# Turning attention probabilities outside TensorE: 32x32 blocks on VectorE and a trip through DRAM in place of identity products, in a two-layer hybrid encoder

## The chip, the core and the metric

The kernel runs on one core of one Trainium2 chip. Times are device microseconds (us) of one execution of the whole program. The core has five engines that run beside each other: TensorE (PE, matrix products; its weight loads are shown as PEld), VectorE (DVE), ScalarE (ACT), GpSimd (POOL) and SyncE (SP). SP does no arithmetic here: it issues nearly all DMAs, in the order of the program, so that a DMA that has to wait for something holds up every DMA behind it on that queue.

## The reference

Two layers. Each has a token mixer and a convolutional MLP, with RMSNorm before each and a residual add behind. SEQ is 256, D_MODEL 1024, everything float32. What matters here is the attention inside the mixer: 12 heads of width 128 in three groups of four, group `g` with window and dilation (128,1), (512,4), (2048,16). The groups' results are combined by their softmax denominators, which is the same as one softmax over the keys of all three groups.

```python
u, q, k, v, g_pool, g_attn = jnp.split(xn @ w_in, SPLITS, axis=-1)
...
logits = jnp.einsum('bqhd,bqkhd->bhqk', qb, kb, preferred_element_type=jnp.float32) * scale
logits = logits + bias.astype(jnp.float32)[None, :, None, :]
logits = jnp.where(valid[None, None], logits, NEG_INF)
lse = jax.nn.logsumexp(logits, axis=-1)
p = jnp.exp(logits - lse[..., None]).astype(vb.dtype)
o = jnp.einsum('bhqk,bqkhd->bqhd', p, vb)
...
wts = jax.nn.softmax(jnp.stack(lses, axis=0), axis=0)
attn = jnp.einsum('gbsh,gbshd->bshd', wts, jnp.stack(outs, axis=0).astype(jnp.float32))
...
merged = jax.nn.sigmoid(g_pool) * (pool_out @ w_a) + jax.nn.sigmoid(g_attn) * (attn_out @ w_b)
return merged @ w_o
```

## The kernel before

**Products and weights.** Most products are made in three parts: both operands are split into a high and a low half in TensorE's fast fp32r type, and high*high, low*high and high*low are summed. Weights come from DRAM in loads of 1 MB into three buffers (`RAW = 3`; `Weights.load`, line 134). Each load is cut into two pieces of 128x1024. ScalarE makes a piece's high half (line 197) and VectorE its low half (line 198); five split pieces can be live (`BUFS = 5`). `Weights.get` asks for the pieces in the order of use, up to `LOOK = 3` ahead of TensorE. `W.loads_behind[n]` puts the issue of load n behind a named DMA on SP's queue, and `W.queue_behind` puts the splitting of some pieces behind named instructions on ScalarE and VectorE.

**Stages of a layer.** (1) values `v`; (2) the pooling branch's input and its projection; (3) queries and keys, six column pairs (`PAIRS`) of four projections each, by `proj` and `two_sums` (matmuls on line 520); (4) the pooling branch times `w_a`, by tokens: `by_tokens(po2, 4)` for two halves of the columns, four pieces each (matmuls on line 644, copied to `pa` on line 1099); (5) two gates for the pooling branch (`gate()`, `by_tokens(x2, 4)`, tanh on line 1107); (6) two gates for attention, each followed by `by_tokens(at2, 2, 2)` with `w_b`; the merged rows are turned to channels by `to_chunks` (lines 663 to 677): a VectorE transpose of 32x32 blocks (line 667), a DMA to DRAM (line 669), four DMAs back (line 671), and the split into halves (line 676); (7) the product with `w_o` (lines 562 to 564) with the residual and the norm; (8) the MLP.

**Attention.** Head `hh` of all three groups is handled at once, in three functions. `scores(hh)` makes for each half `t` of the tokens 128 x 512 logits: 256 columns for the first group (line 985, three parts) and 128 for each of the others (line 990, plain float32). VectorE adds the bias (line 996) and finds the maximum (line 1001), ScalarE makes the exponentials (line 1004), VectorE divides (lines 1006 and 1007). The result `probs[hh, t]` has queries on partitions. `turn(hh)` brings the keys onto partitions: TensorE multiplies each 128x128 block with the identity (line 1019, eight for a head); from PSUM, ScalarE copies the first group's part to `pth` in fp32r (line 1020), VectorE makes its low half `ptl` (line 1025), and the other groups' part is copied to `pt` in float32 (lines 1022 and 1024). `weigh(hh)` multiplies with the values (line 1036 in three parts, line 1040 in plain float32) and splits the result into `at2` (lines 1045 and 1046).

**Where attention stands.** These functions are not a stage of their own. A list `steps` holds twelve of them, in the order scores a, turn a, scores b, weigh a, turn b, weigh b for the pairs of heads (0, 1) and (2, 3). `step()` runs the next one; I call each place where it is called a visit. There is a visit after every second projection of the last three column pairs in stage 3 (six visits), and after six of the eight pieces in stage 4.

**Buffers that the change touches.** Tiles with one tag share memory, one after another. `ybig` holds in turn half of the pooled input (`pl2`), `pa`, and a piece of `w_up`; `xn` holds the other half of `pl2`, the low halves of queries and keys (`qkl`), and the normed rows; `gates` holds `vl` and then the tanh rows `th`; `gain` holds a norm's gain, sent to all partitions by a 512 KB DMA.

Of the kernel before, what the change touches and what calls it, by code (L numbers as in the profile page):

```python
# [10 lines left out]
F32 = mybir.dt.float32  # L11
# [5 lines left out]
P = 128  # L17
D = 1024
S = 256
DEPTH = 2  # L20
KD = D // P
HD = 128
HPG = 4
# [203 lines left out]
def encoder(ctx, tc, x, w_in, w_pool, pool_scale, w_a, w_b, w_o, norm1, norm2, w_up, conv_w,  # L227
            conv_b, w_down, rel_bias, norm_f, onehot, edges, out):
    nc = tc.nc
    const = ctx.enter_context(tc.tile_pool(name="const", bufs=1))  # L230
    wpool = ctx.enter_context(tc.tile_pool(name="weights", bufs=1))
    big = ctx.enter_context(tc.tile_pool(name="big", bufs=1))
    sm = ctx.enter_context(tc.tile_pool(name="small", bufs=2))
    acc = ctx.enter_context(tc.tile_pool(name="acc", bufs=4, space=bass.MemoryType.PSUM))
    mmp = ctx.enter_context(tc.tile_pool(name="mmp", bufs=4, space=bass.MemoryType.PSUM))
    dram = ctx.enter_context(tc.tile_pool(name="dram", bufs=1, space=bass.MemoryType.DRAM))


    W = Weights(tc, wpool, big)

    def cols(w, c0):

        src = w[:, c0 : c0 + 256].rearrange("(k p) c -> p k c", p=P)
        return W.add(
            src, (8, 256), [((lambda t, j=j: t[:, :, j * P : (j + 1) * P]), (8, P)) for j in (0, 1)]
        )
# [10 lines left out]
    first_up = []  # L257
    for l in range(DEPTH):
        for g in range(NG):
            c0 = C_V + g * 512  # L260
            slots = (("m2", 0, 2), ("m2", 1, 2), ("ybig",), ("at2",)) if g == 0 else ()
            for j in range(2):
                tag = "k1" if l == 0 and g == 1 and j == 0 else None
# [25 lines left out]
        for j in range(2):  # L289
            tag = None if j else "k1"  # L290
            W.use(rows(w_up[l], j * 512, 4, 0, 512, tag), slots[2 * j : 2 * j + 2])
        for f in range(0, NF, 2):
            a = cols(w_up[l], f * P) if f >= ENTRY else []
            g = cols(w_up[l], DFF + f * P)
# [10 lines left out]
    def gain(src):  # L305
        g = sm.tile([P, D], F32, tag="gain", bufs=1, name="gain")
        nc.sync.dma_start(out=g, in_=src.partition_broadcast(P))
        return g

    ident = const.tile([P, P], F32, name="ident")  # L310
# [324 lines left out]
    def v_tile():  # L635
        return acc.tile([P, 512], F32, tag="acc", name="v_ps")

    def v_sum(ps, x2, t, n, piece, last=3):


        _, (wh, wl) = piece
        passes = [(0, wh, 0), (0, wl, 0), (1, wh, 0), (0, wh, 1), (0, wl, 1), (1, wh, 1)]
        for m, (part, w, j) in enumerate(passes):
            nc.tensor.matmul(  # L644
                ps, x2[:, 2 * n + j, part, t, :], w[:, j, :], start=(n + m == 0),
                stop=(n == last and m == 5),
            )

    def by_tokens(x2, n, at_once=1, then=None):

        ps = [mmp.tile([P, 512], F32, tag="mm", name="t_ps") for _ in range(2)]
        for i0 in range(0, n, at_once):
            held = [W.get() for _ in range(at_once)]
            for t in range(2):
                for i, piece in enumerate(held, i0):
                    v_sum(ps[t], x2, t, i, piece, n - 1)
            for i, _ in held:
                W.free(i)
            if then:
                then()  # L660
        return ps
# [17 lines left out]
    def two_parts(tag, name):  # L679


        return big.tile([P, KD, 2, 2, P], F32R, tag=tag, name=name)
# [174 lines left out]
    for l in range(DEPTH):  # L857
# [4 lines left out]
        v = big.tile([P, 2, 2 * 512], F32, tag="v1", name="v")  # L862
# [16 lines left out]
        if l == 0:  # L879
            with tc.manual_schedule():  # L880
                begun = begin_values_of_x()
            x2 = first_values(*begun, keep_values)
        else:
            for g in range(NG):
                held = begun[0] if g == 0 else [W.get() for _ in range(4)]
                for t in range(2):
                    if g + t == 0:
                        ps = begun[1]
                    else:
                        ps = v_tile()  # L890
# [6 lines left out]
        if l == 0:  # L897
            load_params()
            with tc.issue_after(W.behind[1].ins):
                bias = build_bias()  # L900
                next(bias)
        g2 = gain(norm2[l])


        pl2 = [
            big.tile([P, KD // 2, 2, 2, P], F32R, tag=tag, name="pl2") for tag in ("ybig", "xn")
# [2 lines left out]
        for gi in range(3, -1, -1):  # L909
# [12 lines left out]
            while sh < w:  # L922
# [3 lines left out]
                    out=nxt[:, :, 0:n], in0=cur[:, :, 0:n], in1=cur[:, :, sh : sh + n]  # L926
# [7 lines left out]
            if hw > 1:  # L934
# [5 lines left out]
                out=pd, in0=cur[:, :, o : o + S], scalar=1.0 / w, in1=u[:, :, PAD : PAD + S],  # L940
# [35 lines left out]
        q = big.tile([P, NH - HPG, 2, P], F32, tag="q1", name="q")  # L976
        kk = big.tile([P, NH - HPG, 2, P], F32, tag="k1", name="k")
        at2 = big.tile([P, HPG, 2, 2, P], F32R, tag="at2", name="at2")
        probs, ptiles = {}, {}

        def scores(hh):
            for t in range(2):
# [26 lines left out]
                )  # L1009
                probs[hh, t] = p  # L1010

        def turn(hh):
            pth = sm.tile([P, 2, 2, P], F32R, tag="pth", bufs=1, name="pth")
            ptl = sm.tile([P, 2, 2, P], F32R, tag="us", name="ptl")
            pt = sm.tile([P, 2, 2, P], F32, tag="pt", bufs=1, name="pt")
            for t in range(2):
                ps = acc.tile([P, 4, P], F32, tag="acc", name="pt_ps")
                for b in range(4):
                    nc.tensor.transpose(ps[:, b, :], probs[hh, t][:, b * P : (b + 1) * P], ident)  # L1019
                nc.scalar.copy(out=pth[:, :, t, :], in_=ps[:, 0:2, :])  # L1020
                if t == 0:
                    nc.scalar.copy(out=pt[:, :, t, :], in_=ps[:, 2:4, :])
                else:
                    nc.vector.tensor_copy(pt[:, :, t, :], ps[:, 2:4, :])
                nc.vector.tensor_sub(
                    out=ptl[:, :, t, :], in0=ps[:, 0:2, :], in1=pth[:, :, t, :].bitcast(F32)
                )
            ptiles[hh] = pth, ptl, pt

        def weigh(hh):  # L1030
            pth, ptl, pt = ptiles[hh]
            ps = acc.tile([P, 2, P], F32, tag="acc", name="o_ps")
            for kc in range(2):
                c = slice(hh * P, (hh + 1) * P)
                for m, (a, b) in enumerate(((vh, pth), (vh, ptl), (vl, pth))):
                    nc.tensor.matmul(ps, a[:, kc, c], b[:, kc], start=(kc + m == 0), stop=False)  # L1036
            for g in (1, 2):
                hd = (g - 1) * HPG + hh
                for t in range(2):
                    nc.tensor.matmul(  # L1040
                        ps[:, t, :], v[:, t, hd * P : (hd + 1) * P], pt[:, g - 1, t, :],
                        start=False, stop=(g == 2 and t == 1),
                    )
            oh, ol = at2[:, hh, 0], at2[:, hh, 1]
            nc.scalar.copy(out=oh, in_=ps)
            nc.vector.tensor_sub(out=ol, in0=ps, in1=oh.bitcast(F32))

        steps = []
        for pair in ((0, 1), (2, 3)):
            a, b = pair  # L1050
            steps += [(scores, a), (turn, a), (scores, b), (weigh, a), (turn, b), (weigh, b)]

        def step():
            if steps:
                f, hh = steps.pop(0)
                f(hh)


        for m, c in enumerate(PAIRS):
            if m == 1:  # L1060
                po2 = two_parts("m2", "po2")
# [5 lines left out]
            for n in range(4):  # L1067
# [3 lines left out]
                hd = 2 * c + n % 2  # L1071
                scale = HD**-0.5 if n < 2 else 1.0
                if hd < HPG:
                    hi, lo = ((qh, ql) if n < 2 else (kh, kl))
                    nc.scalar.mul(out=hi[:, hd], in_=src, mul=scale)
                    nc.vector.scalar_tensor_tensor(
                        out=lo[:, hd], in0=src, scalar=scale, in1=hi[:, hd].bitcast(F32),
# [3 lines left out]
                        out=lo[:, hd], in0=rest, scalar=scale, in1=lo[:, hd].bitcast(F32),  # L1081
                        op0=ALU.mult, op1=ALU.add,
                    )
                else:
# [3 lines left out]
                        out=o, in0=src, scalar=scale, in1=o, op0=ALU.mult, op1=ALU.add  # L1088
# [2 lines left out]
                    step()  # L1091


        pa = big.tile([P, 2, D], F32, tag="ybig", name="pa")
        places = iter(range(KD))
        for cc in HALVES:
            ps = by_tokens(po2, 4, then=lambda: step() if next(places) not in (1, 5) else None)
            for t in range(2):
                nc.scalar.copy(out=pa[:, t, cc], in_=ps[t])
        assert not steps  # L1100


        def gate():
            th = big.tile([P, 2, 512], F32, tag="gates", name="gates")
            ps = by_tokens(x2, 4)
            for t in range(2):
                nc.scalar.activation(th[:, t], ps[t], AF.Tanh, scale=0.5)
            return th

        for cc in HALVES:  # L1110
            th = gate()
            for t in range(2):
                nc.vector.scalar_tensor_tensor(
                    out=pa[:, t, cc], in0=th[:, t], scalar=1.0, in1=pa[:, t, cc],
                    op0=ALU.add, op1=ALU.mult,
                )
# [4 lines left out]
        for n, cc in enumerate(HALVES):  # L1121
            th = gate()
            ps = by_tokens(at2, 2, 2)
            ks = slice(4 * n, 4 * n + 4)
            y = big.tile([P, 2, 4, 4, 32], F32, tag=("q0", "k0")[n], name="turned")
            z = big.tile([P, 2, 4, 4, 32], F32, tag=("q1", "v0")[n], name="merged")
            for t in range(2):

                with tc.issue_after((turned if t else made[1]).ins) if n + t else ExitStack():
                    nc.vector.scalar_tensor_tensor(  # L1130
                        out=th[:, t], in0=th[:, t], scalar=1.0, in1=ps[t], op0=ALU.add, op1=ALU.mult
                    )
                    nc.vector.tensor_add(out=th[:, t], in0=th[:, t], in1=pa[:, t, cc])
                turned, there, made = to_chunks(
                    th[:, t], y[:, t], z[:, t], (mh[:, ks, t], ml[:, ks, t])
                )
# [12 lines left out]
        x2 = two_parts("x", "x2")  # L1149
# [41 lines left out]
        held, ps = entry  # L1191
        first = keep_entry(ps)
        ps = v_tile()
# [70 lines left out]
        if l + 1 < DEPTH:  # L1264
            x2 = two_parts("x", "x2")
# [34 lines left out]
```

## Time and profile before

| | us |
|---|---|
| median of the runs shown (3) | 873.15 |
| lowest and highest of these | 872.96, 873.58 |
| the profiled execution, its own time | 872.91 |
| the profiled execution, its span | 871.1 |
| PE busy in that span | 863.8 |
| DVE, ACT, POOL busy | 661.8, 509.6, 32.6 |

The span runs from the first to the last instruction of the profile. The time includes what lies around it, here 1.8 us. Busy times of PE are modelled from the instruction and overlap a little, since matmuls are pipelined: one matmul's own duration is longer than its distance from the next. The chain of work that ended last gives that distance, and it is the better measure of what a matmul costs.

### The profile page before, as it was taken

How to read it: one execution, taken by the hardware profiler on the slowest of the kernel's cores; microseconds unless marked ns; L12 is line 12 of the kernel's file. 1: busy time of each engine (PE TensorE's matmuls, PEld its weight loads, DVE VectorE, ACT ScalarE, POOL GpSimd, SP SyncE). 2: the span in 40 equal slices, each digit the busy share in tenths (PEclk: the TensorE clock that was granted, in tenths of full speed). 3: DMA queues.
4: the chain of work that ended last, by engine and by line, in shares of the span. 5: the costliest groups of instructions: out<-in, count | busy, mean ns of one | idle time of the engine just before them, and what ended most of it. 6: DMA issues, size and time to landing. Idle time of an engine off the chain costs nothing.

```text
span 871.1 us, 12179 instructions
## 1 busy us (share of the span) xinstructions
PE 863.8 (99%) x4583; PEld 744.5 (85%) x4583; DVE 661.8 (76%) x1070; ACT 509.6 (58%) x847; POOL 32.6 (4%) x98
## 2 busy tenths in 40 slices
PE   9999999999999999999999999999999999999997
PEld 8888898888888888888888888988888888888886
DVE  7998785656769978878855987766567798887884
ACT  7756554544547766666545674545444586666663
POOL 1800000000010000000000000000000100000000
PEclk9999999999999999999999999999999999999999
DMA  9676545545655466475636565455567346556541
GB/s 334 235 248 203 184 148 176 189 165 187 231 187 193 161 225 195 158 229 194 241 122 216 171 215 172 146 163 177 193 226 255 134 155 224 190 173 214 194 145 49
DMA packets 119427, 165.86 MB, mean 190 GB/s; under 512 B 3960, under 2 KB 86592, under 8 KB 119368
## 3 DMA queue, kind: packets, MB, share of 16 engines
q1 hardware_dynamic: 119208, 164.81, 56.4%
q8 instruction: 36, 0.59, 0.3%
q10 hardware_dynamic: 160, 0.27, 0.1%
q14 instruction: 23, 0.19, 0.1%
HBM read 161.90 MB, written 3.17 MB: 189 GB/s over the span
## 4 chain that ended last, share of the span: by engine, by line
PE 98%; DVE 1%; issue 0%; POOL 0%; ACT 0%; POOLq 0%; ACTq 0%
PE proj_ps L520 46%; PE t_ps L644 18%; PE v_ps L644 6%; PE res_ps L564 6%; PE res_ps L563 6%; PE res_ps L562 6%; PE v_ps L849 3%; PE v_ps L756 1%; PE pool_ps L520 1%; PE pt_ps L1019 1%; PE o_ps L1040 1%; PE s_ps L990 1%; PE s_ps L985 1%; PE o_ps L1036 1%; PE xt_ps L458 0%
## 5 line engine op out<-in xcount | busy, mean ns | idle before, releaser
L198 DVE TENSOR_TENSOR wl<-raw,wh 128x1024 fp32r<-128x1024 f32 x274 | 333.1, 1221 | 135.2 <-ACT wh L197 94.7
L197 ACT CAST wh<-raw 128x1024 fp32r<-128x1024 f32 x274 | 286.4, 1050 | 132.8 <-PE t_ps L644 61.6
L520 PE MATMUL proj_ps<-x,wh 128*128 128x512 f32 x1152 | 274.5, 390 | 0.0
L520 PEld LDWEIGHTS proj_ps<-x,wh 128*128 128x128 f32 x1152 | 213.1, 188 | 42.2
L520 PEld LDWEIGHTS proj_ps<-x,wl 128*128 128x128 f32 x1152 | 144.9, 191 | 3.6
L520 PE MATMUL proj_ps<-x,wl 128*128 128x256 f32 x1152 | 147.9, 283 | 0.0
L644 PE MATMUL t_ps<-wh,x 128*128 128x512 f32 x256 | 79.6, 390 | 0.0
L562 PE MATMUL res_ps<-wh,actq 128*128 128x512 f32 (+1 forms) x184 | 70.0, 380 | 0.0
L563 PE MATMUL res_ps<-wl,actq 128*128 128x512 f32 (+1 forms) x184 | 69.9, 380 | 0.0
L564 PE MATMUL res_ps<-wh,actk 128*128 128x512 f32 (+1 forms) x184 | 69.9, 380 | 0.0
L644 PEld LDWEIGHTS t_ps<-wh,x 128*128 128x128 f32 x256 | 48.1, 188 | 9.9
L644 PE MATMUL t_ps<-wl,x 128*128 128x512 f32 x128 | 49.8, 389 | 0.0
L644 PE MATMUL t_ps<-wh,po 128*128 128x512 f32 x128 | 42.7, 399 | 0.0
L563 PEld LDWEIGHTS res_ps<-wl,actq 128*128 128x128 f32 x184 | 34.6, 188 | 6.6
L562 PEld LDWEIGHTS res_ps<-wh,actq 128*128 128x128 f32 x184 | 34.6, 188 | 6.6
L564 PEld LDWEIGHTS res_ps<-wh,actk 128*128 128x128 f32 x184 | 34.6, 188 | 6.5
L1226 ACT ACTIVATE y<-y 128x256 f32<-128x256 f32 x44 | 18.2, 418 | 28.7 <-DVE y L1217 28.6
L431 POOL TENSOR_SCALAR ss<-ss 128x1 f32<-128x1 f32 x8 | 2.2, 273 | 794.9 <-ACT junk L424 794.9
L1213 ACT ACTIVATE y<-a,prm 128x256 f32<-128x256 f32 x36 | 21.6, 601 | 14.5 <-DVE a L557 14.5
L644 PEld LDWEIGHTS t_ps<-wl,x 128*128 128x128 f32 x128 | 24.0, 188 | 5.0
L644 PEld LDWEIGHTS t_ps<-wh,po 128*128 128x128 f32 x128 | 24.1, 188 | 4.8
L424 ACT ACTIVATE junk<-h 128x512 f32<-128x512 f32 (+1 forms) x19 | 10.5, 553 | 27.7 <-DVE h L422 27.7
(209 smaller groups left out, 1184.8 us busy)
## 6 DMA issues: line engine op xcount, KB each, us to landing
raw<-in_w_in_dram SPq DMA_DIRECT2D x58, 1024.0 KB, 5.2
raw<-in_w_up_dram SPq DMA_DIRECT2D x44, 1024.0 KB, 6.7
raw<-in_w_down_dram SPq DMA_DIRECT2D x22, 1024.0 KB, 5.0
raw<-in_w_a_dram SPq DMA_DIRECT2D x8, 1024.0 KB, 5.0
raw<-in_w_o_dram SPq DMA_DIRECT2D x8, 1024.0 KB
raw<-in_w_b_dram SPq DMA_DIRECT2D x4, 1024.0 KB
raw<-in_w_pool_dram SPq DMA_DIRECT2D x2, 1024.0 KB
turned<-turned SPq DMA_DIRECT2D x8, 256.0 KB
```

The source lines that it names most:

```text
L197: lambda: nc.scalar.copy(out=h, in_=src),
L198: lambda: nc.vector.tensor_sub(out=l, in0=src, in1=h.bitcast(F32)),
L424: nc.scalar.activation(junk[:, 0 : cc.stop - cc.start], h[:, t, cc], AF.Square, scale=D**-0.5, accum_out=ss[:, n : n + 1],)
L520: nc.tensor.matmul(out, w(k), x, start=(steps is first and k == 0), stop=(steps is last and k == nk - 1), skip_group_check=turns["rest"],)
L562: nc.tensor.matmul(ps, ah, wh, start=first, stop=False, skip_group_check=on)
L563: nc.tensor.matmul(ps, ah, wl, start=False, stop=False, skip_group_check=on)
L564: nc.tensor.matmul(ps, al, wh, start=False, stop=last, skip_group_check=on)
L644: nc.tensor.matmul(ps, x2[:, 2 * n + j, part, t, :], w[:, j, :], start=(n + m == 0), stop=(n == last and m == 5),)
L756: return nc.tensor.matmul(ps[t], a[:, k, t, :], w[:, k % 2, :], start=first, stop=last)
L849: nc.tensor.matmul(ps[t], a[:, k, t, :], w[:, j, :], start=(k + m == 0), stop=(k == KD - 1 and m == 2),)
L1213: nc.scalar.activation(y, a, AF.Identity, bias=b, scale=w1)
L1226: nc.scalar.activation(y2, y, AF.Square, scale=float(np.sqrt(0.044715)))
```

## The change

`turn` is divided. `start_turn(hh)` takes the probabilities right behind the softmax: two VectorE transposes in 32x32 blocks (one for each half of the tokens), one DMA of 512 KB to DRAM, and four DMAs of 128 KB back into `turned_p`, which put each block in its place. `turn(hh)` is left with one ScalarE copy (the high half) and one VectorE subtraction (the low half), both out of SBUF and both for a whole head; the second and third groups' probabilities are read by `weigh` where they lie, in runs of 32 elements. The identity products on line 1019 and the PSUM copies behind them are gone.

The list of twelve steps becomes a table from a visit's number to what is run there: visits 0 to 5 lie in stage 3, 6 to 13 behind the eight pieces of stage 4, and 14 and 15 behind the first two pieces of the first gate in stage 5. Eight of the visits end in TensorE work (four `scores`, four `weigh`).

Three buffers move with it: `turned_p` takes `ybig`, `pa` takes `xn`, and the blocks on their way to DRAM (`turning`) take `gain`, so that the second norm's gain is now fetched behind the first gate instead of ahead of stage 2. `th` is allocated behind the gate's products. In each `start_turn` one later weight load is put behind its DMAs on SP's queue, and for head 3 the first load of `w_up` too.

```diff
-        g2 = gain(norm2[l])
...
+        turned_p = big.tile([P, 2, 2 * 4, 4, 32], F32, tag="ybig", name="turned_p")
+
+        def start_turn(hh):
+            y = sm.tile([P, 2, 4, 4, 32], F32, tag="gain", bufs=1, name="turning")
+            for t in range(2):
+                nc.vector.transpose(out=y[:, t].rearrange("p q c j -> p c q j"), in_=probs[hh, t])
+            d = dram.tile([2 * P, 4, P], F32, tag="turning", bufs=2, name="turning")
+            nc.sync.dma_start(
+                out=d.rearrange("(t p) q x -> p t (q x)", t=2),
+                in_=y.rearrange("p t q c j -> p t (q c j)"),
+            )
+            z = turned_p[:, hh % 2]
+            for q in range(4):
+                there = nc.sync.dma_start(
+                    out=z[32 * q : 32 * q + 32].rearrange("p a c j -> p a (c j)"),
+                    in_=d[:, q].rearrange("(a i) x -> i a x", i=32),
+                )
+            W.loads_behind[W.n_loaded + 1] = there
+            if hh == HPG - 1:
+                W.loads_behind[first_up[l][1]] = there
+
         def turn(hh):
+            z = turned_p[:, hh % 2]
             pth = sm.tile([P, 2, 2, P], F32R, tag="pth", bufs=1, name="pth")
             ptl = sm.tile([P, 2, 2, P], F32R, tag="us", name="ptl")
-            pt = sm.tile([P, 2, 2, P], F32, tag="pt", bufs=1, name="pt")
-            for t in range(2):
-                ps = acc.tile([P, 4, P], F32, tag="acc", name="pt_ps")
-                for b in range(4):
-                    nc.tensor.transpose(ps[:, b, :], probs[hh, t][:, b * P : (b + 1) * P], ident)
-                nc.scalar.copy(out=pth[:, :, t, :], in_=ps[:, 0:2, :])
-                if t == 0:
-                    nc.scalar.copy(out=pt[:, :, t, :], in_=ps[:, 2:4, :])
-                else:
-                    nc.vector.tensor_copy(pt[:, :, t, :], ps[:, 2:4, :])
-                nc.vector.tensor_sub(
-                    out=ptl[:, :, t, :], in0=ps[:, 0:2, :], in1=pth[:, :, t, :].bitcast(F32)
-                )
-            ptiles[hh] = pth, ptl, pt
+            hi, lo = (p.rearrange("p c t (a j) -> p (t a) c j", j=32) for p in (pth, ptl))
+            nc.scalar.copy(out=hi, in_=z[:, :, 0:2])
+            nc.vector.tensor_sub(out=lo, in0=z[:, :, 0:2], in1=hi.bitcast(F32))
+            ptiles[hh] = pth, ptl, z
...
-                        ps[:, t, :], v[:, t, hd * P : (hd + 1) * P], pt[:, g - 1, t, :],
+                        ps[:, t, :], v[:, t, hd * P : (hd + 1) * P], pt[:, 4 * t : 4 * t + 4, 1 + g, :],
...
-        steps = []
-        for pair in ((0, 1), (2, 3)):
-            a, b = pair
-            steps += [(scores, a), (turn, a), (scores, b), (weigh, a), (turn, b), (weigh, b)]
+        steps = {
+            0: ((scores, 0), (start_turn, 0)),
+            2: ((scores, 1), (start_turn, 1)),
+            3: ((turn, 0),),
+            4: ((weigh, 0),),
+            6: ((turn, 1), (scores, 2), (start_turn, 2)),
+            7: ((weigh, 1),),
+            8: ((scores, 3), (start_turn, 3)),
+            12: ((turn, 2),),
+            13: ((weigh, 2),),
+            14: ((turn, 3),),
+            15: ((weigh, 3),),
+        }
+        places = iter(range(20))
         def step():
-            if steps:
-                f, hh = steps.pop(0)
+            for f, hh in steps.pop(next(places), ()):
                 f(hh)
...
-        pa = big.tile([P, 2, D], F32, tag="ybig", name="pa")
-        places = iter(range(KD))
+        pa = big.tile([P, 2, D], F32, tag="xn", name="pa")
         for cc in HALVES:
-            ps = by_tokens(po2, 4, then=lambda: step() if next(places) not in (1, 5) else None)
+            ps = by_tokens(po2, 4, then=step)
...
         def gate():
+            ps = by_tokens(x2, 4, then=step if steps else None)
             th = big.tile([P, 2, 512], F32, tag="gates", name="gates")
-            ps = by_tokens(x2, 4)
...
             th = gate()
+            if cc.start == 0:
+                g2 = gain(norm2[l])
```

More of the change, by code (lines that the diff above doesn't have):

```diff
@@ L1091, in encoder @@
                     step()
-        pa = big.tile([P, 2, D], F32, tag="ybig", name="pa")
-        places = iter(range(KD))
+        pa = big.tile([P, 2, D], F32, tag="xn", name="pa")
         for cc in HALVES:
-            ps = by_tokens(po2, 4, then=lambda: step() if next(places) not in (1, 5) else None)
+            ps = by_tokens(po2, 4, then=step)
             for t in range(2):
                 nc.scalar.copy(out=pa[:, t, cc], in_=ps[t])
-        assert not steps
         def gate():
+            ps = by_tokens(x2, 4, then=step if steps else None)
             th = big.tile([P, 2, 512], F32, tag="gates", name="gates")
-            ps = by_tokens(x2, 4)
             for t in range(2):
@@ L1111, in encoder @@
             th = gate()
+            if cc.start == 0:
+                assert not steps
+                g2 = gain(norm2[l])
             for t in range(2):
```

## The prediction

> **What bounds the kernel now.** I read the page's span, busy times and chain first, then the waits in order of size, then the engines' busy time by stage.
>
> ```profile
> span 871.1 us, 12179 instructions
> PE 863.8 (99%) x4583; PEld 744.5 (85%) x4583; DVE 661.8 (76%) x1070; ACT 509.6 (58%) x847; POOL 32.6 (4%) x98
> ...
> PE 98%; DVE 1%; issue 0%; POOL 0%; ACT 0%; POOLq 0%; ACTq 0%
> ```
>
> The chain that ended last is TensorE for 98% of the span: an instruction taken from TensorE shortens the kernel by its share of the chain, as long as nothing else comes late. The waits say what stands nearest.
>
> ```profile
> ACT wh L197 <- PE t_ps L644: 61.6, 40, 2.5
> ...
> ACT wh L197 <- DMA raw<-in_w_up_dram: 6.7, 5, 1.9
> ...
> ACT wh L197 <- DMA raw<-in_w_in_dram: 1.6, 1, 1.6
> ...
> PEld res_ps L564 <- DVE m L676: 0.6, 2, 0.3
> ```
>
> ScalarE, which starts each weight's split, waits 61.6 us for TensorE to free a piece and hardly for a load: weights come faster than TensorE uses them. The only wait of TensorE near this change is 0.3 us in each layer, for the merged rows.
>
> ```profile
> 107.50:143.50 36.00, 36.00 (x233) 32.73 (x233) 27.17 (x51) 18.99 (x37) 0.00 (x0) 1.00 0.44 147
> 143.50:173.80 30.30, 30.30 (x169) 26.08 (x168) 19.41 (x33) 15.85 (x29) 0.00 (x0) 1.00 0.57 188
> ...
> 228.20:267.40 39.20, 38.82 (x198) 32.45 (x198) 27.81 (x38) 19.76 (x32) 2.81 (x7) 1.00 0.55 182
> ...
> 658.00:697.00 39.00, 38.62 (x198) 32.33 (x197) 27.64 (x38) 19.60 (x32) 2.82 (x7) 1.00 0.55 184
> ```
>
> The columns are the stretch, its length, then PE, PEld, DVE, ACT and POOL busy, the granted clock and the DMA share. In the first layer's attention (first two rows) TensorE is never idle, VectorE is busy 27.17 + 19.41 = 46.6 us of 66.3, and the DMA engines half. The last two rows hold the product with w_o: TensorE idles 0.38 us in each.
>
> **The change part by part.** *The identity products go.* The chain in order of time shows what they cost.
>
> ```profile
> 107.48 0.36 PE s_ps L985 x3
> ...
> 109.08 5.57 PE proj_ps L520 x32
> 114.65 0.87 PE pt_ps L1019 x8
> 115.53 5.55 PE proj_ps L520 x32
> ...
> 128.26 0.71 PE o_ps L1036 x6
> 128.96 0.89 PE o_ps L1040 x8
> ...
> 135.41 0.87 PE pt_ps L1019 x8
> ...
> 143.46 2.75 PE t_ps L644 x12
> ...
> 153.30 1.04 PE pt_ps L1019 x8
> ...
> 168.55 0.88 PE pt_ps L1019 x8
> ...
> 544.19 0.87 PE pt_ps L1019 x8
> ...
> 564.94 0.87 PE pt_ps L1019 x8
> ...
> 582.83 1.03 PE pt_ps L1019 x8
> ...
> 598.07 0.88 PE pt_ps L1019 x8
> ```
>
> Two layers of four heads of eight products; the groups sum to 0.87 + 0.87 + 1.04 + 0.88 + 0.87 + 0.87 + 1.03 + 0.88 = **7.31 us**, all on the path. The products around them do not lengthen (5.57 before the group, 5.55 behind).
>
> *VectorE and ScalarE.*
>
> ```profile
> L198 DVE TENSOR_TENSOR wl<-raw,wh 128x1024 fp32r<-128x1024 f32 x274 | 333.1, 1221 | 135.2 <-ACT wh L197 94.7 <-PE proj_ps L520 38.9
> L197 ACT CAST wh<-raw 128x1024 fp32r<-128x1024 f32 x274 | 286.4, 1050 | 132.8 <-PE t_ps L644 61.6 <-PE res_ps L564 29.3 <-PE proj_ps L520 28.1
> ...
> L1025 DVE TENSOR_TENSOR ptl<-pt_ps,pth 128x256 fp32r<-128x256 f32 x16 | 6.6, 414 | 0.0
> ...
> L1020 ACT CAST pth<-pt_ps 128x256 fp32r<-128x256 f32 x16 | 6.1, 380 | 0.1
> ...
> L667 DVE STREAM_TRANSPOSE turned<-gates 128x512 f32<-128x512 f32 x8 | 5.7, 712 | 0.3
> ...
> L676 DVE TENSOR_TENSOR m<-merged,m 128x512 fp32r<-128x512 f32 x8 | 5.5, 684 | 0.0
> ...
> L676 ACT CAST m<-merged 128x512 fp32r<-128x512 f32 x8 | 4.8, 618 | 0.0
> ...
> L1024 DVE COPY pt<-pt_ps 128x256 f32<-128x256 f32 x8 | 3.3, 412 | 0.0
> ...
> L1022 ACT COPY pt<-pt_ps 128x256 f32<-128x256 f32 x8 | 3.0, 380 | 0.0
> ```
>
> The first two rows are a weight's split, for later. The merged rows already take the route that the probabilities are to take (lines 667 to 676, same shapes and the same runs of 32), so every new instruction has a row. VectorE gains 16 transposes of 0.712 and 8 subtractions of 0.684, 16.9 us, and loses 6.6 + 3.3: +7.0 us in all, 3.5 in a layer. ScalarE gains 8 copies of 0.618 and loses 6.1 + 3.0: -4.2 us. Both lie beside TensorE: 46.6 + 3.5 = 50.1 us of VectorE in the 62.7 that are left of the stage. I cost them at nothing; without that cover they would cost those 3.5 us in each layer.
>
> [...] The rows above say which engine has room here: TensorE none, VectorE 66.3 - 46.6 = 19.7 us. [...]
>
> *The trip through DRAM.* It takes time, and SP's queue stands behind it.
>
> ```profile
> 112.80 0.89 DVE L1007 TENSOR_SCALAR p<-p,rz 128x512 f32<-128x512 f32 x2
> ```
> ```profile
> 148.90 0.37 SPq L134 DMA_DIRECT2D raw<-in_w_in_dram  x1
> ```
> ```profile
> 211.38 0.34 SPq L669 DMA_DIRECT2D turned<-turned  x1
> 213.44 1.97 SPq L671 DMA_DIRECT2D merged<-turned  x4
> ```
> ```profile
> DMA to landing us min/median/max: 1.8/2.4/3.6
> ```
> ```profile
> raw<-in_w_in_dram SPq DMA_DIRECT2D x58, 1024.0 KB, 5.2
> ```
>
> A softmax ends 112.80 + 0.89 - 109.08 = 4.6 us behind its scores; two transposes make 1.4; the first read is issued 2.06 us behind the write; four issues take 2.0; the reads of 64 KB land 1.8 to 3.6 us later (those of 128 KB are not in this trace: I take 3.6). That is 4.6 + 1.4 + 2.1 + 2.0 + 3.6 = 13.7 us from the scores' end to a turned head. Now the places, with visits 5.56 us apart up to the sixth, 2.75 from there, and 1.60 for each `scores` or `weigh`. Scores of head 0 end at 109.1, of head 1 at 109.1 + 2 x 5.56 + 1.60 = 121.8, of head 2 (after `weigh` 0, three more column pairs' visits and one pass) at 121.8 + 3 x 5.56 + 1.60 + 2.75 + 1.60 = 144.4, of head 3 (after `weigh` 1 and two passes) at 144.4 + 2 x 2.75 + 2 x 1.60 = 153.1; the turn is asked for at 127.3, 142.8, 164.1 and 171.2. That leaves 18.2, 21.0, 19.7 and **18.1 us**, all above 13.7. Head 3 is the tightest. In VectorE's order one weight split (1.22) stands inside its softmax: 153.1 + 4.6 + 1.2 + 1.4 puts its write at 160.3 and its data at 160.3 + 2.1 + 2.0 + 3.6 = 168.0. Its copy (0.62) and subtraction (0.68) then stand behind head 2's `weigh`, which ends at 168.5, and behind two weight splits that follow that, and end near 173.1; TensorE's `weigh` for head 3 stands at 174.0. I take no wait, with 1 us to spare. Queued behind the copy on ScalarE are the splits of the next weights, and TensorE would wait for those next.
>
> *SP's queue.* The write of a head waits for VectorE, and what is queued behind it waits too. In the order of the changed kernel the longest such hold is that of the load with the first gate's second half (issued at 148.90 before): it stands behind head 2's reads and head 3's write, so at 160.7. TensorE needs its piece at 175.6; ahead of that lie 5.2 (landing) and 1.05 + 1.22 (the split on ScalarE and on VectorE), so the last moment for the issue is 168.1. That is 7.4 us to spare, and the cost is nothing. The three buffers and five live pieces are what hides it.
>
> *Reading in runs.* `weigh` now reads its float32 operand in runs of 32 elements, 64 products at 0.89 / 8 = 0.111 us each. No row here shows such a read by TensorE. Between 0 and, at half the rate, 64 x 0.111 = 7.1 us; I take 0, since the nearest row is ScalarE's copy on line 676, which goes through the same runs of 32 with 512 elements in 0.618 us, where two copies of 256 without such runs (line 1020) take 2 x 0.380. I keep 7.1 as a rival.
>
> *The rest.* The later norm gain (512 KB) is used only behind the product with w_o, whose stretch begins at 228.20, over 40 us after its new place. A piece of w_up may be split earlier, as `ybig` comes free sooner: VectorE and ScalarE then have one piece less to do ahead of the merged rows, whose wait costs TensorE 0.38 us a layer at most. Between 0 and -0.76; I take 0.
>
> *Sum*, against the profiled execution's own 872.91: 872.91 - 7.31 = **865.6**. That execution lies 0.24 below the median of 873.15, well within the runs.
>
> **The rivals.** *A, the turned head comes late.* In the changed order a 1 MB weight load is issued between the write and the reads of heads 1 and 3. If the reads' data waits for it, head 3 lands at 160.7 + 5.2 + 3.6 = 169.5, still ahead of its copy near 171. Should the softmax or the load be 3 to 5 us slower than worked out, `weigh` waits 1 to 3 us, in both layers: 865.6 + 2 to 6, about **869**. For it: 1 us to spare at the end. Against: 18 us against 13.7 ahead of that.
>
> [...]
>
> *B, slower: weights starve behind the writes.* The same hold, priced differently: each us by which that load is issued after 168.1 costs TensorE a us, in each layer. It ends above the time before once it passes 168.1 + 7.31 / 2 = 171.8, over 11 us later than worked out. At 16 us late it is 2 x (16 - 7.4) = 17.2, so 865.6 + 17.2 = **883**. For it: SP holds everything behind a wait. Against: weights wait for TensorE now, not the reverse.
>
> *C, TensorE reads short runs at half rate:* 865.6 + 7.1 = **872.7**, no difference.
>
> *D, the change doesn't do what it says:* TensorE's time is freed but weights, ScalarE or VectorE set the pace, and the same time comes back as waits: **872.9**. Against: the 61.6 us of waits for TensorE.
>
> **How the numbers follow.** Forecast 0.76, A 0.12, B 0.05, C 0.04, D 0.03. Low end: 872.91 - 7.31 - 0.76 = 864.8, and 0.4 for runs that differ by 0.6. High end: A up to 869.5. That leaves out B, C, D and the top of A, 0.17 in all. A measurement of this kernel can tell about 0.2% (1.75 us) from no change. Faster: the forecast and nearly all of A, 0.87; same: C, D and a little of A, 0.08; slower: B, 0.05.
>
> **What would show it.** Right: no L1019, the chain still 98% TensorE with two layers' attention 3.7 us shorter each, o_ps groups at 0.71 and 0.89, no wait of TensorE for the turned copies. A would show as waits of o_ps for ScalarE or VectorE, longest at head 3; B as ScalarE's splits waiting for weight loads, and then TensorE; C as o_ps groups of 1.8. The forecast is wrong if VectorE's queue runs later than I place it: its splits and transposes share one order, and I placed them by hand.

## The result, and the profile after

The changed kernel takes 864.23 us (median of 4 runs, 863.86 to 864.36) against 873.06 us for the kernel before on the same chip (4 runs): a ratio of 0.9898, 95% interval 0.9881 to 0.9915, **8.8 us faster**. The forecast was 865.6, a gain of 7.31: direction and mechanism hold, and the gain is 1.5 us larger than forecast and 0.17 us beyond the low end of the range. The question of this section and the next is where those 1.5 us come from.

The page of the kernel after, its span, busy times and chain:

```profile
span 862.6 us, 12111 instructions
PE 855.9 (99%) x4519; PEld 738.2 (86%) x4519; DVE 665.2 (77%) x1070; ACT 506.6 (59%) x831; POOL 32.6 (4%) x98
...
PE 99%; DVE 0%; ACT 0%; issue 0%; POOL 0%; POOLq 0%; ACTq 0%
```

TensorE has 64 products fewer (4583 to 4519), and the chain is now TensorE alone: the 1% of VectorE that stood in it before is gone. That is the first trace of the surplus: the identity products were TensorE's, not VectorE's.

The chain in order of time, after, at the end of attention in both layers (start, length, what):

```profile
177.21 0.89 PE o_ps L1056 x8
178.10 46.51 PE t_ps L644 x205
...
603.27 46.51 PE t_ps L644 x205
```

The same view of the kernel before:

```profile
173.76 54.44 PE t_ps L644 x240
...
603.29 54.44 PE t_ps L644 x240
...
696.90 30.58 PE proj_ps L520 x176
```

Weighing moved later (178.10 instead of 173.76), with 35 of the gates' products moved ahead of it, so only the end of the run of products can be compared: 173.76 + 54.44 = 228.20 before, 178.10 + 46.51 = 224.61 after, 3.59 us, and 3.71 with the 0.12 us by which the run after reached attention later (107.60 against 107.48). The identity products take 3.65 to 3.66 in a layer by the prediction's rows, so this is they and little else. In the second layer attention starts at 537.01 before and 532.77 after, and the same marks give (603.29 + 54.44 - 537.01) - (603.27 + 46.51 - 532.77) = 120.72 - 117.01 = 3.71 again: 2 x 3.71 = 7.4 of the 8.8.

The rest lies behind attention. The stretch from the first product with w_o to the long run of MLP projections (`res_ps` to `proj_ps`) in the stage view, after, in both layers:

```profile
224.61:263.15 38.54, 38.54 (x199) 32.50 (x198) 27.78 (x37) 18.87 (x31) 2.39 (x7) 1.00 0.58 194
649.78:688.30 38.52, 38.52 (x198) 32.49 (x198) 27.77 (x37) 18.86 (x30) 2.37 (x7) 1.00 0.59 199
```

The prediction's row for this stretch before, 228.20:267.40, has 39.20 us, with TensorE idle for 0.38. After, it is 38.54 us and never idle: 0.66 us less. In the second layer the same marks are 603.29 + 54.44 = 657.73 and 696.90 before, 39.17 us, against 38.52 after: 0.65 less, so 1.3 us in both. The waits of the kernel before name the place (columns: sum, times, longest):

```profile
PEld v_ps L644 <- DVE x L462: 1.6, 2, 0.8
PE v_ps L644 <- DVE x L462: 0.8, 2, 0.4
```

After, neither row is there. Line 462 makes the low half of the normed, turned rows `x` that the MLP multiplies first. TensorE and VectorE at that point, before:

```profile
250.93 0.71 PE L644 MATMUL v_ps<-v,x 128*128 128x512 f32 x2
252.02 1.20 PE L644 MATMUL v_ps<-v,x 128*128 128x512 f32 x4 [0.38 <-DVE x L462]
253.06 1.53 PE L644 MATMUL v_ps<-ybig,x 128*128 128x512 f32 x6
```
```profile
250.16 1.21 DVE L198 TENSOR_TENSOR wl<-raw,wh 128x1024 fp32r<-128x1024 f32 x1
251.29 0.68 DVE L462 TENSOR_TENSOR x<-xt_ps,x 128x512 fp32r<-128x512 f32 x1
```

and after:

```profile
247.15 1.64 PE L644 MATMUL v_ps<-v,x 128*128 128x512 f32 x6
248.63 1.07 PE L644 MATMUL v_ps<-ybig,x 128*128 128x512 f32 x4
```
```profile
246.39 0.68 DVE L462 TENSOR_TENSOR x<-xt_ps,x 128x512 fp32r<-128x512 f32 x1
246.98 1.21 DVE L198 TENSOR_TENSOR wl<-raw,wh 128x1024 fp32r<-128x1024 f32 x1
```

Before, VectorE splits a weight (1.21 us) ahead of `x`; after, it makes `x` first. Nothing in the diff says so: the scheduler that lays out each engine's order came out another way. From the first of the six products to the first of the next six is 253.06 - 250.93 = 2.13 us before and 248.63 - 247.15 = 1.48 after, 0.65 less (2.13 and 1.47 in the second layer). The idle time beside the row is only 0.38: the first two products are recorded as 0.71 us, though two without a wait are 2 x 1.48 / 6 = 0.49 apart from what follows. **A product's recorded duration reaches past the point at which the next could have started (six without a wait, after: 1.64 us recorded, 1.48 to the next), so TensorE's idle time of 0.38 us understates what the wait cost, 0.65.**

### The profile page after: what moved, and what is told of

Its sections match the earlier page's. It is cut to its first block, busy times and chain, and to the rows that moved or that the text cites. A ratio compares the mean times of both kernels' runs of the same rounds, so it can differ in the third digit from the quotient of the medians.

```text
span 862.6 us, 12111 instructions
## 1 busy us (share of the span) xinstructions
PE 855.9 (99%) x4519; PEld 738.2 (86%) x4519; DVE 665.2 (77%) x1070; ACT 506.6 (59%) x831; POOL 32.6 (4%) x98
## 4 chain that ended last, share of the span: by engine, by line
PE 99%; DVE 0%; ACT 0%; issue 0%; POOL 0%; POOLq 0%; ACTq 0%
PE proj_ps L520 46%; PE t_ps L644 18%; PE v_ps L644 6%; PE res_ps L562 6%; PE res_ps L563 6%; PE res_ps L564 6%; PE v_ps L849 3%; PE v_ps L756 1%; PE pool_ps L520 1%; PE o_ps L1056 1%; PE s_ps L988 1%; PE s_ps L983 1%; PE o_ps L1052 1%; PE xt_ps L458 1%; PE gain_ps L349 0%; PE xt_ps L704 0%
```

## The experiments

**Theory 1**: the gain has two parts, the identity products (7.3 to 7.5 us) and VectorE's order at the normed rows (0.65 us in each layer, 1.3), and the trip through DRAM adds nothing. **Theory 2**: the second part has another cause. In e2 that is the weight piece split earlier because `pa` left `ybig`, which my prediction had named; elsewhere it is whatever else the change brings. Medians of before in the two groups of runs are 873.07 (e1 to e4) and 873.20 (e5 to e8).

**e1: the kernel before with the order alone.** A call in `to_channels` puts the split (its halves on ScalarE and on VectorE) behind `x`:

```diff
+                    if n == 0 and t == 0 and psum is acc:
+                        W.queue_behind(last, 1, first_up[l][0] + 3)
```

> The kernel before, with one thing changed behind the product with w_o: the low half of the normed rows' first quarter (VectorE, line 462) stands ahead of the split of the fourth piece of w_up in VectorE's order, as it does in the changed kernel. Theory 1 (the 1.3 us that the prediction missed come from this order: TensorE waits for that low half): 1.0 to 1.3 us less than before, so 871.8 to 872.1, and TensorE's 0.38 us of idle time in each layer gone. Theory 2 (they come from VectorE having one piece of w_up less to split there, since the buffer ybig is free sooner): no difference, 873.1. Theory 3 (chance of a schedule's alignment, no cause of its own): within 0.3 us of before.

871.85 us, ratio 0.9987 (0.9978 to 0.9996): -1.2 us, with 0.3 to 1.9 for the interval. In its trace the six products run through:

```profile
251.19 1.63 PE L646 MATMUL v_ps<-v,x 128*128 128x512 f32 x6
252.66 1.52 PE L646 MATMUL v_ps<-ybig,x 128*128 128x512 f32 x6
```

252.66 - 251.19 = 1.47, as after, and 1.48 in the second layer. Identity products and old turning are all still there: the order alone is worth about 1.2.

**e2: the kernel before with `pa` in the other buffer**, so that the piece of `w_up` can be split earlier, as in after.

```diff
-        pa = big.tile([P, 2, D], F32, tag="ybig", name="pa")
+        pa = big.tile([P, 2, D], F32, tag="xn", name="pa")
```

> The kernel before, with one part of the change alone: pa lies in xn instead of ybig, so that ybig is free sooner and its piece of w_up is split earlier. TensorE still turns the probabilities. VectorE's order at the normed rows is that of before. Theory 1 (order): 0 to 0.4 us less (only the merged rows' wait can go), so 872.7 to 873.1. Theory 2 (one split less): 1.3 us less, 871.8.

873.19 us, ratio 1.0003 (0.9995 to 1.0012): no difference, and both waits for `x` stay at 1.6 and 0.8. The explanation that my prediction had offered for a gain of up to 0.76 falls.

**e3: after, with the split ahead of `x` again**, forced through `issue_after`.

```diff
+                if split_first:
+                    W._split(first_up[l][0] + 4)
+                with tc.issue_after(W.last_lo.ins) if split_first else ExitStack():
+                    last.append(nc.vector.tensor_sub(out=ol, in0=pt, in1=oh.bitcast(F32)))
```

> The changed kernel, with the split of the fourth piece of w_up put ahead of the low half of the normed rows' first quarter on VectorE, as it stood before. Theory 1 (order): 0.9 to 1.3 us more than the changed kernel's 864.2, so 865.1 to 865.5, with TensorE's 0.38 us idle time in each layer back. Theory 2 (one split less): no difference, 864.2.

864.41 us, ratio 0.9897 (0.9884 to 0.9911): no loss. That is theory 2's number, and against theory 1 as I had put it. The trace shows when `x` was ready:

```profile
247.24 1.64 PE L646 MATMUL v_ps<-v,x 128*128 128x512 f32 x6
248.72 1.07 PE L646 MATMUL v_ps<-ybig,x 128*128 128x512 f32 x4
```
```profile
245.80 1.22 DVE L198 TENSOR_TENSOR wl<-raw,wh 128x1024 fp32r<-128x1024 f32 x1
246.94 0.68 DVE L465 TENSOR_TENSOR x<-xt_ps,x 128x512 fp32r<-128x512 f32 x1
```

The split does stand first, but the scheduler moved two additions to `h` (0.34 us each) behind `x` in exchange, and `x` ends at 246.94 + 0.68 = 247.62, 0.38 us behind the first product's start. The third product is the first that needs it. So the order by itself is no loss; being late is. e6 was made to settle that.

**e4: the kernel before without turning.** The probabilities go into `pth`, `ptl` and `pt` as they lie, with queries on partitions; the identity products are left out, so this kernel leaves out the transposition that attention needs. Buffers, splits and copies stay.

```diff
-                ps = acc.tile([P, 4, P], F32, tag="acc", name="pt_ps")
-                for b in range(4):
-                    nc.tensor.transpose(ps[:, b, :], probs[hh, t][:, b * P : (b + 1) * P], ident)
+                ps = probs[hh, t].rearrange("p (b x) -> p b x", b=4)
```

> The kernel before without the turn: the 64 identity products are left out, and the copies behind them take the probabilities as they are, queries on partitions, so the weighing uses unturned probabilities. It prices the identity products alone, with no trip through DRAM and with the before's twelve visits and VectorE order. All theories of the gain on TensorE: 7.3 to 7.4 us less, 865.7. If the removal brings the rest too (theory 2 or another that hangs on the products): 8.6 us or more less, 864.5 or below. If the trip costs the changed kernel something unseen: lower than the changed kernel's 864.2 plus its order's 1.3.

865.36 us, ratio 0.9909 (0.9896 to 0.9923): -7.7 us, with the waits for `x` still at 1.6 and 0.8. This is what the turning costs when nothing takes its place. With e1's 1.2 it makes 8.9, and the change brings 8.8 (the two intervals reach 1.2 and 0.8 us either way): the trip through DRAM, the 16 VectorE transposes and the reading in runs of 32 cost nothing that these runs can tell.

**e5: after without the holds on SP's queue** (the loads that `start_turn` puts behind its DMAs). This tests a step of the prediction, and gives a clean return of the old order as a by-product.

```diff
-            W.loads_behind[W.n_loaded + 1] = there
-            if hh == HPG - 1:
-                W.loads_behind[first_up[l][1]] = there
```

> After without the two holds of SP's loads behind the trip (start_turn's entries in loads_behind); the trip itself stays. A by-product: VectorE's order at the normed rows falls back to the one of before, the weight split (wl) ahead of the low half of x. Theory 1 (the part of the gain above the identity products, some 1.3 us of 8.8, is VectorE's order at the normed rows; the hold costs nothing): 864.2 + 1.3 = 865.5 us, with TensorE's waits on x (1.6 and 0.8 us in two layers) back. Theory 2 (that part is from somewhere else in the change): 864.2, or under it if the hold costs anything.

866.03 us, ratio 0.9918 (0.9905 to 0.9932): +1.8 over after, where theory 1 had 1.3. The order is back, and with it the loss, 249.58 - 247.44 = 2.14 us for the six:

```profile
247.44 0.71 PE L644 MATMUL v_ps<-v,x 128*128 128x512 f32 x2
248.54 1.20 PE L644 MATMUL v_ps<-v,x 128*128 128x512 f32 x4 [0.39 <-DVE x L462]
249.58 1.53 PE L644 MATMUL v_ps<-ybig,x 128*128 128x512 f32 x6
```

The other 0.4 or so is a wait of attention itself, in the second layer, for head 2's turned rows:

```profile
592.16 0.62 ACT L1039 CAST pth<-turned_p 128x512 fp32r<-128x512 f32 x1 [0.98 <-DMA turned_p<-turning]
```
```profile
592.84 0.38 PE L1049 MATMUL o_ps<-pth,vh 128*128 128x256 f32 x1
...
593.57 0.38 PE L1049 MATMUL o_ps<-ptl,vh 128*128 128x256 f32 x1
```

Without the holds, weight loads go onto the queue ahead of the trip's DMAs (in the first layer 1 MB at 117.48 and at 153.26 us, between the write and the reads of heads 0 and 2). The reads take longer from issue to landing in e5 (minimum, median, longest; in the first layer head 0's 5.3 and head 2's 4.7) than after, where heads 0 and 2 take 2.5 and 2.6 (below). In the second layer, where TensorE waits, the chain of e5 has 8.92 us from the issue of head 2's last read to the copy that waits for it; after, it is 3.8 (581.5 to 585.3).

```profile
DMA to landing us min/median/max: 4.7/5.2/5.7
```

So the holds, which I had only asked for what they cost, bring about 0.4 us: this is rival A, the turned head that comes late, in small.

**e6: e3 with one more copy on VectorE ahead of `x`** (128x512 of `h` into a tile that nobody reads).

```diff
+                    with tc.issue_after(late.ins):
+                        junk = sm.tile([P, 512], F32, tag="s", name="junk")
+                        late = nc.vector.tensor_copy(out=junk, in_=h[:, t, 0:512])
```

> After with the weight split and one more copy of 128x512 on VectorE (its result is read by nobody) ahead of the low half of x, so that it ends past 248.0 us where the third product of the normed rows needs it at 247.7. Theory 1: TensorE waits on x again, 0.4 to 0.9 us a layer, 865.0 to 866.0 us. Theory 2 (the order is no cause): 864.2 to 864.5, as e3.

864.77 us, ratio 0.9904 (0.9890 to 0.9918): +0.5, below the expected 0.8 to 1.8, since the copy took less time than I had reckoned (it moved `x` by 0.33 us). The interval overlaps that of after, so what decides is the trace:

```profile
247.03 1.97 PE L651 MATMUL v_ps<-v,x 128*128 128x512 f32 x6
248.84 1.53 PE L651 MATMUL v_ps<-ybig,x 128*128 128x512 f32 x6
```
```profile
246.73 0.42 DVE L468 COPY junk<-h 128x512 f32<-128x512 f32 x1
247.06 0.69 DVE L470 TENSOR_TENSOR x<-xt_ps,x 128x512 fp32r<-128x512 f32 x1
```

With it four kernels stand in one line, first layer, all from the rows above:

| kernel | `x` ends, behind the first product's start | the six take | lost against after |
|---|---|---|---|
| after | 246.39 + 0.68 - 247.15 = -0.08 | 1.48 | 0 |
| e3 | 247.62 - 247.24 = 0.38 | 1.48 | 0 |
| e6 | 247.06 + 0.69 - 247.03 = 0.72 | 1.81 | 0.33 |
| before | 251.29 + 0.68 - 250.93 = 1.04 | 2.13 | 0.65 |

In the second layer the six take 1.47, 1.48, 1.81 and 2.13. In these four kernels 0.38 us of lateness cost nothing, and 0.34 and 0.66 us beyond it cost 0.33 and 0.65. That is what e3 had hidden, and it settles the surplus: 2 x 0.65 = 1.3 us.

**e7: after with the identity products put back**, eight for each head, of the identity itself, into a PSUM tile that nobody reads. The trip stays, so this kernel has both; the order at the normed rows falls back as well.

```diff
+            for t in range(2):
+                ps = acc.tile([P, 4, P], F32, tag="acc", name="pt_ps")
+                for b in range(4):
+                    nc.tensor.transpose(ps[:, b, :], ident, ident)
```

> After with eight identity products of 128x128 a head put back beside the trip (64 in all, of the identity, into a PSUM tile that nobody reads). VectorE's order at the normed rows falls back to the one of before. Theory 1: the products cost 7.2 to 7.5 us and the order 1.3, 872.6 to 873.1 us. Theory 2 (the products alone): 871.4 to 871.7. If the trip or VectorE's block transpositions had hidden a cost or a gain of their own, the sum would miss the time of before by as much.

872.92 us, ratio 1.0000 (0.9991 to 1.0009): the time of before, as theory 1 adds it up, and above what the products alone would give. The trip stands beside TensorE at no cost and for no gain of its own.

**e8: attention pressed together.** Heads 2 and 3 are turned and weighed at visits 10 to 12, and later products are held behind the weighing.

```diff
-            12: ((turn, 2),),
-            13: ((weigh, 2),),
-            14: ((turn, 3),),
-            15: ((weigh, 3),),
+            10: ((turn, 2),),
+            11: ((weigh, 2), (turn, 3)),
+            12: ((weigh, 3),),
```

> After with the turning and weighing of heads 2 and 3 moved to visits 10 to 12, and TensorE's later products held behind the weighing, so that head 3 is weighed some 12 us after its scores' end instead of 23. The trip's data land at 167.0 to 169.4 by the issues and durations of after, the first product can run 0.6 us later, and TensorE would be there at some 164.8 us: a wait of 2.8 to 5.2 us a layer. With the order at the normed rows falling back (1.3): 864.2 + 1.3 + 5.6 to 10.4 = 871 to 876 us. If the trip were quicker than its rows say, 865.5.

877.99 us, ratio 1.0047 (1.0035 to 1.0060): slower than before, 13.8 us over after and 2 us above what I expected. The waits are the size I had worked out:

```profile
168.64 0.38 PE L1055 MATMUL o_ps<-pth,vh 128*128 128x256 f32 x1 [2.46 <-ACT pth L1045]
169.74 0.58 PE L1055 MATMUL o_ps<-ptl,vh 128*128 128x256 f32 x1 [0.71 <-DVE ptl L1046]
...
170.97 1.91 PE L1059 MATMUL o_ps<-turned_p,v 128*128 128x128 f32 x8
172.53 0.75 PE L647 MATMUL t_ps<-wh,po 128*128 128x512 f32 x1
```
```profile
600.90 0.58 PE L1055 MATMUL o_ps<-pth,vh 128*128 128x256 f32 x1 [3.30 <-ACT pth L1045]
```

What is new is the row with 1.91: after, the same eight products are recorded as 1.05. The stage view of TensorE (stretch, length, busy, granted clock, DMA share, GB/s) shows why:

```profile
165.90:168.64 2.74, 0.28 (x3) 1.00 0.98 294
168.64:170.50 1.86, 1.15 (x4) 0.79 0.97 345
170.50:172.50 2.00, 2.00 (x12) 0.50 1.03 386
172.50:173.40 0.90, 0.90 (x5) 0.65 1.05 389
173.40:176.00 2.60, 2.60 (x13) 1.00 1.06 420
```

Behind the gap the granted clock is 0.50 for 170.50 to 172.50, and in the chain the eight plain products take 1.71 us instead of 0.89. Taken as one fall from 1.00 to 0.50 and one return, the rows put the fall at 169.7 us (0.79 over 1.86 us) and the return at 173.1 (0.65 over 0.90): 3.4 us. Behind the gap of 3.30 in the second layer the products are as slow, up to 606.68, where two products in a row are recorded as 0.62 again:

```profile
602.87 1.91 PE L1059 MATMUL o_ps<-turned_p,v 128*128 128x128 f32 x8
...
605.42 1.05 PE L647 MATMUL t_ps<-wh,po 128*128 128x512 f32 x2
606.28 0.56 PE L647 MATMUL t_ps<-wl,po 128*128 128x512 f32 x1
606.68 0.62 PE L647 MATMUL t_ps<-wh,po 128*128 128x512 f32 x2
```

What the slow products cost is read from the distances between starts, against the same products of head 2 in e8's second layer, which run at their usual distance:

```profile
593.09 0.39 PE L1055 MATMUL o_ps<-ptl,vh 128*128 128x256 f32 x1 [0.20 <-DVE ptl L1046]
...
595.14 0.63 PE L647 MATMUL t_ps<-wh,po 128*128 128x512 f32 x2
...
595.84 0.63 PE L647 MATMUL t_ps<-wh,po 128*128 128x512 f32 x2
```

In the first layer they take 173.36 - 169.74 = 3.62 us instead of 595.14 - 593.09 = 2.05, in the second 606.68 - 601.63 = 5.05 instead of 595.84 - 593.09 = 2.75: 1.6 and 2.3 us more, so here a wait of about 3 us cost half to seven tenths as much again. Gaps of 2.46 + 0.71 + 3.30 = 6.5, the slow products with 3.9 and the order with 1.3 make 11.7 of the 13.8, and idle time understates the waits, as above. One of e8's nine executions took 872.70 us at a mean granted clock of 0.998, the others 876.60 to 878.38 at 0.992 to 0.996. The 5.3 us between it and the median are more than the 3.9; whether it waited as long as the others is not shown, since there is no trace of it.

The data's delay is not the reads' alone. In the first layer head 3's copy on ScalarE stood behind two weight splits whose load came late (6.36 us in the chain from its issue to the split at 165.64); only in the second did it wait for the reads, for 1.5 us. So the change lives from the distance that its table leaves. After, head 3 is weighed from here on:

```profile
175.64 0.28 PE L1052 MATMUL o_ps<-pth,vh 128*128 128x256 f32 x1
```

That is 22.5 us behind its scores' end (153.1 in the prediction, 153.26 in the chain after); in e8 TensorE stands ready at 168.64 - 2.46 = 166.2, 13 us behind them.

## Why the prediction was right or wrong, point by point

- **TensorE is the bound: right.** The chain is TensorE for 98% and then 99%, and e1, e4 and e7 move the time by what they move on TensorE.
- **Identity products, 7.31 us, all on the path: right.** 2 x 3.71 = 7.4 by the marks of the two traces, 7.7 (interval 6.7 to 9.1) by e4.
- **VectorE and ScalarE at no cost: right**, e7. VectorE's busy time rose by 665.2 - 661.8 = 3.4 us instead of 7.0, which mattered to nothing. In this kernel the products on TensorE cost 7.7 us (e4), and the way over VectorE costs nothing that the runs can tell (e7).
- **The trip, 13.7 us from scores to a turned head: right within a us.** SP's rows after, for heads 0 and 3:

```profile
115.05 0.37 SPq L1021 DMA_DIRECT2D turning<-turning  x1
117.83 1.83 SPq L1027 DMA_DIRECT2D turned_p<-turning  x4
...
158.91 0.38 SPq L1021 DMA_DIRECT2D turning<-turning  x1
159.38 0.41 SPq L134 DMA_DIRECT2D raw<-in_w_in_dram  x1
162.03 1.80 SPq L1027 DMA_DIRECT2D turned_p<-turning  x4
```

  and the landing of the reads of heads 0, 1 and 2 in the first layer, then of head 3 in the second, each from a window of its own:

```profile
DMA to landing us min/median/max: 2.5/2.5/2.5
```
```profile
DMA to landing us min/median/max: 6.0/6.0/6.0
```
```profile
DMA to landing us min/median/max: 2.6/2.6/2.6
```
```profile
DMA to landing us min/median/max: 4.6/4.6/4.6
```

  Head 0's scores end at 109.21 (the next group of projections starts there), and 117.83 + 1.83 + 2.5 - 109.21 = 13.0 us. The reads followed the write by 2.8 and 3.1 us instead of 2.06 (the write has 512 KB, the row I had taken 256). Heads 1 and 3, with a 1 MB load issued between write and reads, wait 6.0 and 4.6 for theirs, the others 2.5 and 2.6; e5 puts a load there for heads 0 and 2 as well, and they wait 5.3 and 4.7. That fits rival A, in which the reads' data wait for the load's. The trace of before has such reads too: its 64 KB reads of the merged rows behind a 1 MB load landed in 3.5 and 3.6 us (loads at 215.98 and 645.29, reads from 217.79 and 647.20), the others in 1.8 to 2.9. A load and reads that only share the rate of the DMA engines would fit as well; no run here tells the two apart. Head 3's write went out at 158.91 (160.3 forecast), and its data came at about 162.03 + 1.80 + 4.6 = 168.4 (168.0 forecast; the landing is that of the second layer). TensorE weighed it at about 175.6, not 174.0, since the scheduler does not hold a visit's work at its place: 32 of the gate's products stand between the two weighings there, where two visits have 24.
- **SP's hold costs nothing: right**, the load was issued at 159.38 (160.7 forecast). ScalarE waited longer for loads of `w_in` (1.6 to 5.6 us), and TensorE did not. That the hold itself brings 0.4 us, e5, I had not seen.
- **Reading in runs of 32 at no cost: right.** The eight plain products of a weighing stand at 0.89 in both chains; rival C is out.
- **"The rest", taken as 0 and bounded at -0.76: the step that failed.** I took TensorE's 0.38 us of idle time behind the product with w_o for the merged rows' wait and for its whole price. The waits view had the answer, in a row above the one I quoted: 1.6 us for `x` against 0.6 for the merged rows. So two things were wrong: the cause (`x` is late, by VectorE's order at the normed rows; e1, e5 and e6 show it, e2 rules out the earlier split), and the size, since idle time shows 0.38 of a loss of 0.65. The term is 1.3 where I allowed 0.76 at most. With it the sum is 872.91 - 7.31 - 1.30 = 864.3. These 1.3 us are luck: nothing in the change was meant to bring them.
- **The rivals.** A, the late turn, did not happen: ScalarE waited for the reads once, 0.3 us, and TensorE not at all. e5 has it in small and e8 in full. My price for it, a us of waiting for a us of time, leaves out the clock, 3.9 us in e8. B, C and D did not happen either.

What stays open: e4 and the marks differ by 0.3 us on the identity products, well within e4's interval. And no run singles out what in the change turned VectorE's order round; it fell back without the holds (e5), with the identity products (e7) and with the other visits (e8).

## What to carry to other kernels

Where one engine is the whole chain, work that can be had on another is worth its place on that engine's path, even at a longer way round, as long as the distance between its making and its use is longer than the way: here a way of 13 to 15 us was free where the use came 22 us behind, and where it came 13 us behind it lost more than the change had won. Read every wait of the bounding engine near the change, largest first, and measure its price as the distance between instructions on either side, not as idle time. And look at how the change leaves each engine's order in places that the diff does not touch: here that was a seventh of the gain.

## What the runs showed of the hardware beyond that

- In e8 the granted clock fell from 1.00 to 0.50 behind gaps of TensorE of 2.46 and 0.71 us, for about 3.4 us by the stage view; behind a gap of 3.30 the eight plain products were recorded as 1.91 us again instead of 1.05, and the usual durations came back at 606.68, 5.8 us after the gap's end. Gaps of 0.38 in before left the clock at 1.00 in the stage view. Which length of gap brings the fall, and what sets its duration, is not shown.
- Reads issued right behind a 1 MB load on the same queue landed 2 to 3.5 us later than those without: 128 KB in 4.6 and 6.0 us against 2.5 and 2.6 after, and in 5.3 and 4.7 in e5, with a load put ahead of the latter two.
